# Which of four tiles the first of the two final plain stores takes

## Chip, cores and metric

One core of one Trainium2 chip. The metric is the device time of one execution in microseconds (us), the median of several runs. Every granted clock is 1.0 (the kernel has no matmul). The profile's own span is about 1.8 us shorter than the time of the run.

## The reference

The input is `x`, 16 x 64 x 64 x 64 float32. All 15 x 15 windows of 8 x 8 at a stride of 4 are copied out, 59.0 MB in all:

```python
for i in range(n_h):
    for j in range(n_w):
        h_start = i * stride
        w_start = j * stride
        result[:, i, j] = x[:, :, h_start:h_start + window_size, w_start:w_start + window_size].copy()
```

## The kernel before

The input is loaded once. Then windows are put together by ACT and DVE (copies, and shuffles for windows that cross a partition) in a tile of 128 partitions by 16 KB, and stored. There is room for four such tiles, G0 to G3. They are dealt in turn by a counter:

```python
NG = 4
G = [gpool.tile([P, C, WS, WS], f32, name=f"G{n}") for n in range(NG)]
...
at = 0

def tile_():
    nonlocal at
    at += 1
    return G[(at - 1) % NG]
```

Most stores are indirect (`scatter`, issued by POOL; each partition's 16 KB row goes to a row of the output that an index names; rows with an index out of bounds are left out). A crossing store (s = 2) leaves out 16 of the 64 rows of one half of the partitions, and `turn` says which half:

```python
def unit(j, s):
    nonlocal crossed
    g = tile_()
    ...
        turn = crossed % 2
        crossed += 1
        fill(g, turn, s, j, 0, HP, (act, act))
        fill(g, 1 - turn, s + 1, j, 0, HP, (dve, dve))
        scatter(g, (idx_hi, idx_lo)[turn], j, s)
...
while plain:
    for w in cross[:3]:
        unit(*w)
    cross = cross[3:]
    unit(*plain.pop(0))
```

The last column of windows (j = 14) is left over: two half-full tiles, 64 rows each, which go out by plain stores, four of 16 rows (256 KB) for each tile. SP issues all four of the first tile and two of the second; ACT issues the other two:

```python
j = NW - 1
tile_()
for s in range(2):
    g = tile_()
    cols = slice(j * ST, j * ST + WS)
    for y in range(NY):
        d = slice(QP + y * QP, QP + (y + 1) * QP)
        for ch, copy in enumerate((act, dve)):
            f = slice(ch * HP + y * QP, ch * HP + (y + 1) * QP)
            copy(out=g[d, ch * CL : (ch + 1) * CL, :, :], in_=L[f, :, s * ST : s * ST + WS, cols])
    g_q = g.rearrange("p c r w -> p (c r w)")
    for q in range(HQ):
        free((nc.sync, nc.scalar)[s * q % 2].dma_start(out=o_q[q * NSLOT + s, j], in_=g_q[QP + q : QP + q + (B - 1) * HQ + 1 : HQ]))
```

Of the kernel before, what the change touches and what calls it, by code (L numbers as in the profile page):

```python
# [10 lines left out]
def kernel(  # L11
# [106 lines left out]
    def free(st):  # L118
        tc.declare_no_dep(st.ins, group="stores", reason="each store writes rows of its own")
        tc.add_to_no_dep_group("stores", st.ins)  # L120
# [31 lines left out]
# [6 lines that stand above are left out]
# [43 lines left out]


    j = NW - 1
    tile_()
    for s in range(2):
        g = tile_()
        cols = slice(j * ST, j * ST + WS)
        for y in range(NY):
            d = slice(QP + y * QP, QP + (y + 1) * QP)
# [6 lines that stand above are left out]
# [35 lines left out]
```

## Time and profile before

| | before |
|---|---|
| time, median of the first 3 runs | 191.89 us |
| span in the profile | 190.1 us |
| DVE busy / ACT busy / POOL busy | 63% / 68% / 26% |
| share of DMA in the chain that ended last | 84% |
| moved over the span | 75.81 MB, 399 GB/s mean |

No compute engine is near its limit; transfers are.

### The profile page before, as it was taken

How to read it: one execution, taken by the hardware profiler on the slowest of the kernel's cores; microseconds unless marked ns; L12 is line 12 of the kernel's file. 1: busy time of each engine (PE TensorE's matmuls, PEld its weight loads, DVE VectorE, ACT ScalarE, POOL GpSimd, SP SyncE). 2: the span in 40 equal slices, each digit the busy share in tenths (PEclk: the TensorE clock that was granted, in tenths of full speed). 3: DMA queues.
4: the chain of work that ended last, by engine and by line, in shares of the span. 5: the costliest groups of instructions: out<-in, count | busy, mean ns of one | idle time of the engine just before them, and what ended most of it. 6: DMA issues, size and time to landing. Idle time of an engine off the chain costs nothing.

```text
span 190.1 us, 481 instructions
## 1 busy us (share of the span) xinstructions
DVE 120.5 (63%) x160; ACT 130.0 (68%) x69; POOL 49.9 (26%) x50
## 2 busy tenths in 40 slices
DVE  4000007999998969877659586795877679552420
ACT  0000007999999989977779589797877979572750
POOL 7402203205535321522322222223122431210000
DMA  2999999999999999999999999999999999999974
GB/s 83 310 408 403 398 400 396 400 401 392 438 431 431 422 424 441 417 410 417 441 397 431 426 422 414 424 438 393 438 414 417 428 424 424 405 434 410 421 331 197
DMA packets 11156, 75.81 MB, mean 399 GB/s; under 512 B 3456, under 2 KB 3456, under 8 KB 7552
## 3 DMA queue, kind: packets, MB, share of 16 engines
q0 software_dynamic: 9040, 66.34, 84.7%
q1 hardware_dynamic: 2048, 8.91, 12.0%
q10 hardware_dynamic: 64, 0.52, 0.7%
q14 instruction: 4, 0.03, 0.0%
HBM read 16.78 MB, written 62.91 MB: 419 GB/s over the span
## 4 chain that ended last, share of the span: by engine, by line
DMA 84%; DVE 6%; ACT 3%; POOL 2%; issue 1%; ACTq 0%; DVEq 0%; PEldq 0%
DMA out_dram<-G,idx_hi 30%; DMA L<-in_x_dram 20%; DMA out_dram<-G,idx 14%; DMA out_dram<-G,idx_y 13%; DMA out_dram<-G,idx_lo 7%; DVE G L166 4%; POOL L L58 2%; ACT G L212 2%; ACT G L143 1%; DVE G L146 1%; DVE G L145 0%; DVE G L143 0%; POOL pi L69 0%; ACTq L143 0%; DVEq L145 0%
## 5 line engine op out<-in xcount | busy, mean ns | idle before, releaser
L143 ACT COPY G<-L 64x2048 f32<-64x2048 f32 x46 | 87.2, 1896 | 17.0 <-DMA out_dram<-G,idx_hi 7.6
L166 DVE COPY G<-L 32x2048 f32<-32x2048 f32 x30 | 36.9, 1230 | 28.9 <-DMA L<-in_x_dram 25.9
L146 DVE STREAM_SHUFFLE G<-L 64x1024 f32<-64x1024 f32 x30 | 38.3, 1276 | 0.0
L166 ACT COPY G<-L 32x2048 f32<-32x2048 f32 x18 | 33.9, 1896 | 1.2 <-DMA out_dram<-G,idx_y 0.8
L145 DVE COPY G<-L 64x1024 f32<-64x1024 f32 x30 | 20.6, 688 | 16.4 <-DMA out_dram<-G,idx_hi 10.5
L143 DVE COPY G<-L 64x2048 f32<-64x2048 f32 x16 | 19.6, 1223 | 6.7 <-DMA out_dram<-G,idx 6.3
L166 ACT ACT_TABLE_LOAD x1 | 1.3, 1283 | 29.5 <-DMA L<-in_x_dram 29.5
L123 POOL DMA_INDIRECT out_dram<-G,idx_y x6 | 10.8, 1808 | 25.2 <-DVE G L166 24.1
L58 POOL DMA_DIRECT2D L<-in_x_dram x16 | 10.9, 695 | 24.1 <-DMA L<-in_x_dram 23.6
L123 POOL DMA_INDIRECT out_dram<-G,idx_hi x8 | 9.7, 1207 | 24.2 <-DVE G L146 12.3
L123 POOL DMA_INDIRECT out_dram<-G,idx_lo x7 | 8.0, 1144 | 29.4 <-DVE G L146 19.6
L123 POOL DMA_INDIRECT out_dram<-G,idx x8 | 10.2, 1270 | 18.0 <-ACT G L143 18.0
L212 ACT COPY G<-L 32x2048 f32<-32x2048 f32 x4 | 7.6, 1897 | 5.5 <-DMA out_dram<-G,idx_lo 4.5
L212 DVE COPY G<-L 32x2048 f32<-32x2048 f32 x4 | 4.9, 1220 | 8.2 <-DMA out_dram<-G,idx_lo 5.8
L72 DVE TENSOR_SCALAR tb<-pi 128x1 int32<-128x1 int32 x1 | 0.2, 155 | 1.0 <-POOL pi L69 1.0
L78 DVE TENSOR_TENSOR th<-tc,tq 128x1 int32<-128x1 int32 x2 | 0.3, 156 | 0.0
L75 DVE TENSOR_SCALAR th<-tc 128x1 int32<-128x1 int32 x2 | 0.3, 154 | 0.0
L69 POOL IOTA pi<- 128x1 int32 x1 | 0.1, 124 | 0.4 <-PEq L246 0.4
L146 DVE LOAD_MASK_SELECT G<-L x30 | 0.2, 6 | 0.0
L78 DVE CUSTOM_DVE_ANT_0 tb<-tb,th 128x2 uint16<-128x2 uint16 x1 | 0.2, 160 | 0.0
L78 DVE CUSTOM_DVE_ANT_0 idx_y<-idx_y,idx 128x2 uint16<-128x2 uint16 x1 | 0.2, 160 | 0.0
L78 DVE CUSTOM_DVE_ANT_0 idx<-tb,th 128x2 uint16<-128x2 uint16 x1 | 0.2, 159 | 0.0
(16 smaller groups left out, 2.2 us busy)
## 6 DMA issues: line engine op xcount, KB each, us to landing
L<-in_x_dram POOLq DMA_DIRECT2D x8, 1024.0 KB, 21.1
L<-in_x_dram SPq DMA_DIRECT2D x8, 896.0 KB
out_dram<-G SPq DMA_DIRECT2D x6, 256.0 KB
L<-in_x_dram POOLq DMA_DIRECT2D x8, 128.0 KB, 21.2
out_dram<-G ACTq DMA_DIRECT2D x2, 256.0 KB
out_dram<-G,idx POOLq DMA_INDIRECT x8, 14.7
out_dram<-G,idx_hi POOLq DMA_INDIRECT x8, 14.6
out_dram<-G,idx_lo POOLq DMA_INDIRECT x7, 12.9
```

What stands on the lines that cost most here:

```text
L58: eng.dma_start(out=L[p0 : p0 + QP - HQ + 1 : HQ, c0:c1, :, :], in_=x_v[ch, y, q, :, c0:c1, :])
L69: nc.gpsimd.iota(pi[:, :], pattern=[[0, 1]], base=0, channel_multiplier=1)
L72: nc.vector.tensor_scalar(out=d[:, :], in0=pi[:, :], scalar1=shift, scalar2=mask, op0=ALU.logical_shift_right, op1=ALU.bitwise_and)
L75: nc.vector.tensor_scalar(out=d[:, :], in0=a[:, :], scalar1=float(m), scalar2=None, op0=ALU.mult)
L78: nc.vector.tensor_tensor(out=d[:, :], in0=a[:, :], in1=b[:, :], op=op)
L123: st = nc.gpsimd.indirect_dma_start(out=o_v, out_offset=bass.IndirectOffsetOnAxis(ap=ix[:, 0:1], axis=0), in_=g.rearrange("p c r w -> p (c ...
L143: copy(out=g[d, cs, :, :], in_=L[f, :, s * ST : s * ST + WS, cols])
L145: copy(out=g[d, cs, 0:ST, :], in_=L[f, :, s * ST : RB, cols])
L146: nc.vector.stream_shuffle(out=g[d, cs, ST:WS, :], in_=L[f, :, 0:ST, cols], mask=nxt)
L166: (act if (2 * d + ch) % 3 == 0 else dve)(out=g[d * QP : (d + 1) * QP, ch * CL : (ch + 1) * CL, :, :], in_=L[f : f + QP, :, s * ST : s * S ...
L212: copy(out=g[d, ch * CL : (ch + 1) * CL, :, :], in_=L[f, :, s * ST : s * ST + WS, cols])
```

## The change

The intent is that the first plain fill should take the tile that comes free next, instead of letting that one go by, so that it doesn't wait. The tile that is passed over is now the one between the two plain fills, so the second fill keeps its tile.

```diff
     j = NW - 1
-    tile_()
     for s in range(2):
         g = tile_()
+        at += 1
```

## The prediction

> **What bounds the kernel now.** I read the page first, then the chain that ended last, then the timeline, the stretches and the DMA queues of the last 35 us, since the change touches nothing earlier: each engine's order of instructions is the same in both builds up to the last two fills.
>
> The chain of work that ended last, in its final part (start us, us, what):
>
> ```profile
> 164.83 14.61 DMA out_dram<-G,idx_hi
> ...
> 179.52 1.90 ACT G L212
> 181.44 1.90 ACT G L212
> ```
>
> The end hangs on one store landing, then on the second of the two plain fills (two ACT copies), then on its store, which the chain does not print: 183.34 to 190.1.
>
> To see who holds which tile I counted the allocations. Tiles are dealt in turn from four, by a counter. Nine uses go to the first nine fills, twenty to the loop, so the last four of the loop are use 25 (G1, idx_hi), 26 (G2, idx_lo), 27 (G3, idx_hi) and 28 (G0, idx). Use 29 (G1) is thrown away, the first plain fill is use 30 (G2), the second is use 31 (G3). The timeline (start us, busy us, engine, line, ..., the idle time before and its releaser):
>
> ```profile
> 155.90 1.24 POOL L123 DMA_INDIRECT out_dram<-G,idx_hi  x1 [3.06 <-ACT G L143]
> ...
> 160.95 0.96 POOL L123 DMA_INDIRECT out_dram<-G,idx_lo  x1 [3.81 <-DVE G L146]
> ...
> 164.83 0.97 POOL L123 DMA_INDIRECT out_dram<-G,idx_hi  x1 [2.93 <-DVE G L146]
> 166.41 3.82 ACT L143 COPY G<-L 64x2048 f32<-64x2048 f32 x2 [2.44 <-DMA out_dram<-G,idx]
> ...
> 170.50 0.96 POOL L123 DMA_INDIRECT out_dram<-G,idx  x1 [4.70 <-ACT G L143]
> 174.68 3.82 ACT L212 COPY G<-L 32x2048 f32<-32x2048 f32 x2 [4.45 <-DMA out_dram<-G,idx_lo]
> ...
> 178.52 7.26 SPq L215 DMA_DIRECT2D out_dram<-G  x6
> 179.52 3.82 ACT L212 COPY G<-L 32x2048 f32<-32x2048 f32 x2 [1.02 <-DMA out_dram<-G,idx_hi]
> ...
> 183.37 1.29 ACTq L215 DMA_DIRECT2D out_dram<-G  x2
> ```
>
> The reader is to see three things. ACT is idle for 4.45 us before the first plain fill, because it waits for G2 (store 26, issued 160.95, landed 174.64). The second plain fill starts when G3 (store 27, issued 164.83) lands at 179.44, and that wait doesn't name G1 or G2 at all. And SP issues six of the eight plain stores in one row, 178.52 to 185.78.
>
> Stretches of the tail (window, length, busy DVE, ACT, POOL, clock, DMA share, GB/s):
>
> ```profile
> 174.00:176.00 2.00, 1.27 (x2) 1.32 (x1) 0.00 (x0) 1.00 1.05 442
> 176.00:178.00 2.00, 1.17 (x1) 1.98 (x2) 0.00 (x0) 1.00 0.92 393
> 178.00:180.00 2.00, 0.47 (x1) 0.98 (x2) 0.00 (x0) 1.00 0.97 410
> 180.00:182.00 2.00, 1.97 (x2) 1.98 (x2) 0.00 (x0) 1.00 0.83 352
> 182.00:184.00 2.00, 0.00 (x1) 1.34 (x1) 0.00 (x0) 1.00 0.68 287
> 184.00:186.00 2.00, 0.00 (x0) 0.00 (x0) 0.00 (x0) 1.00 0.93 393
> 186.00:188.00 2.00, 0.00 (x0) 0.00 (x0) 0.00 (x0) 1.00 0.78 328
> 188.00:190.10 2.10, 0.00 (x0) 0.00 (x0) 0.00 (x0) 1.00 0.02 8
> ```
>
> Until 180 the transfers fill the 16 engines; after that they are not quite full, and the last 2.1 us are landing only. The queues in 180 to 182 (queue, packets, MB, share):
>
> ```profile
> q0 software_dynamic: 35, 0.46, 54.0%
> q1 hardware_dynamic: 31, 0.25, 29.3%
> ```
>
> This is how the plain stores (q1, issued by SP) and the indirect ones (q0, issued by POOL) share: 0.25 of 0.71 MB goes to q1.
>
> **What the Trainium skill says.** "DMA: Bandwidth & Descriptors", section "Queues, rings and completion order": each DMA engine goes round between the queues that have work, packet by packet. The trace agrees (q0 and q1 both move in 180 to 182). So an earlier plain store isn't put behind the queued indirect stores; it takes bandwidth from them. Same page, section "Why a DMA increments its semaphore by 16 and not by 1": a transfer has landed only when all of its engines have finished; so store 27's slowest engine counts. Here a store lands some 3 us after its bytes are through on average (worked out below). Same page, "Anatomy of one DMA": about 2 us of a transfer are fixed, mostly the receipt. The last 2.1 us at 8 GB/s agree. Same page, "Issuing engines are not separate DMA queues": issuing from several engines saves only issue time. So no bandwidth is gained here either.
>
> **The change part by part.** Removed: nothing. Added: nothing. The sums of bytes, copies and stores are equal. Moved: the first plain fill goes from use 30 (G2) to use 29 (G1). The second one stays on G3, since the counter is stepped once more after the first.
>
> (a) First fill. It now waits for store 25 instead of 26. Store 25 was issued at 155.90; with the usual 14.6 us of idx_hi to landing it lands near 170.5. (Stores 24 and 26 land at 166.37 and 174.64, so the middle is 170.5 too.) ACT is through with the fill before it at 166.41 + 3.82 = 170.23. So the first fill starts near 170.5 instead of 174.68, 4.2 us earlier, and SP issues its four stores from 174.4 instead of 178.52. The first packets followed the issue by about 1.4 us (178.52 to about 179.9 in the half-microsecond stretches): from 175.8. None of these 4.2 us is on the path to the end as such.
>
> (b) Second fill. It needs store 27. In 178 to 184 q0 moved 0.80 + 0.46 + 0.20 = 1.46 MB, all of it store 28's, whose size is 128 rows of 16 KB = 2.10 MB. So 0.64 MB of 28 had gone by 178, and the bytes of 27 were through on average at 178 - 0.64/0.41 = 176.4, yet it landed only at 179.44. From 175.8 the first plain store now takes its 0.125 MB per us (0.25 MB in 2 us, above). On the slowest engine 27 is still moving until about 177.5 to 178.5 (1 to 2 us of receipt before 179.44). That is 1.7 to 2.7 us by 0.125 = 0.2 to 0.34 MB put ahead, or 0.5 to 0.8 us at 0.41 MB per us; up to twice that if the slowest engine gets the unlucky share; less if most of the lag is receipt. I take +0.8 us, within 0 to 1.6. The second fill then ends at 184.15 instead of 183.34.
>
> (c) The end. Before, SP's fifth store waited its turn: filled 183.34, issued 183.77, and q1 still carried the first plain store until about 185.3. Now SP and q1 are free by then (174.4 + 5.1 us of four issues = 179.5), so the second store's issue and packets come 0.4 to 0.8 us sooner after its fill. I take -0.6 us.
>
> Sum: +0.8 - 0.6 = +0.2 us: 192.1 us.
>
> **The rivals.** First, the bytes simply move up and the end gets the gap. The tail from 178 moved 3.56 MB (the sum of the six stretches). At 0.415 MB per us it would take 8.6 us, ending at 186.6, plus 2.0 of landing: 188.6, so at most 1.5 us (0.8%) faster: 190.4 us. Against it: the second store can't start before store 27 lands, and the change doesn't bring that nearer; the gain is limited to (c). Second, the earlier store delays 27 by its whole size: 1.05 MB at 0.41 = 2.5 us, of which (c) gives back 0.6: 193.8 us, 1% slower. Against it: 27's bytes are mostly through by the time, and q1 gets only about a third. Third, nothing at all: 27's lag is receipt, and SP's backlog is harmless because the DMA engines share the end anyway: 191.9 us.
>
> **Range and chances.** The low end is no delay and 0.7 of (c): 191.2. The high end is a delay of 1.6 or somewhat more and little of (c): 193.2. Two per cent are 3.8 us; faster by that is more than the whole gap in the tail holds (1.5 us), slower by that is more than a delay by the store's whole size. So within 2% is nearly sure, 0.97; faster 0.01, slower 0.02.
>
> **What would show it.** Right: ACT's idle time before the first L212 copies shrinks from 4.45 us to under 0.6 and its releaser is idx_hi; SP's first plain store is issued near 174.4; the second pair of L212 copies starts at 179.5 to 181.1 still released by idx_hi, after a longer idle time of ACT; q1 moves about 1 MB in 176 to 182 and q0's share falls there; SP's last two issues follow the fill at once. Wrong: the second fill starts later than 181.5, which would mean that q1 takes more than a third or that the slowest engine decides; or the second store takes longer from issue to the end than the 6.8 us of before (183.34 to 190.1), with indirect bytes still in q0 then; or the first fill doesn't start by 171, so that store 25 landed later than worked out.

## The result, and the profile after

| | before | after |
|---|---|---|
| time, median of 6 runs each | 191.94 us (191.54 to 192.29) | 192.15 us (191.97 to 192.41) |
| ratio, after to before | | 1.0012, 95% interval 0.9998 to 1.0026 |

A ratio is the mean time of one kernel's runs over that of the other's in the same rounds, so it is not quite the ratio of the medians. Executions over 1.5% slower than the fastest of the same kernel are left out of the means. By the interval, 0.2 us slower is not told apart from nothing.

The same views as before, for the changed kernel. The chain that ended last (start us, us, what):

```profile
165.08 14.62 DMA out_dram<-G,idx_hi
...
179.78 1.90 ACT G L212
181.70 1.90 ACT G L212
```

It is the chain of before, 0.26 us later in all. Those 0.26 us arose ahead of the change: store 27 (idx_hi, G3) was issued at 165.08 instead of 164.83, where both kernels still have the same instructions. It took 14.62 us to land, against 14.61. The spans of the two profiles differ by 0.55 us; the other 0.29 us came after the last packet (0.54 us to the last landing instead of 0.37, and 1.04 us from there to the end instead of 0.92).

The timeline (start us, busy us, engine, line, and the idle time before with its releaser):

```profile
170.76 0.96 POOL L123 DMA_INDIRECT out_dram<-G,idx  x1 [4.71 <-ACT G L143]
171.31 3.81 ACT L212 COPY G<-L 32x2048 f32<-32x2048 f32 x2 [0.82 <-DMA out_dram<-G,idx_hi]
...
175.15 10.28 SPq L215 DMA_DIRECT2D out_dram<-G  x6
179.78 3.82 ACT L212 COPY G<-L 32x2048 f32<-32x2048 f32 x2 [4.66 <-DMA out_dram<-G,idx_hi]
...
183.62 1.83 ACTq L215 DMA_DIRECT2D out_dram<-G  x2
```

ACT's idle time of 4.45 us ahead of the first plain fill has shrunk to 0.82; that fill starts at 171.31 instead of 174.68. The idle time has moved: ACT now stands 4.66 us ahead of the second plain fill, which waits for the same landing as before.

Now the queues (q0 holds the stores that POOL issues, q1 those of SP, q10 those of ACT): what moved in 176 to 178, 178 to 180 and 180 to 182 (the first line is the first of these stretches, and so on; queue, packets, MB, share of the engines):

```profile
q0 software_dynamic: 56, 0.92, 107.9%
...
q0 software_dynamic: 52, 0.72, 84.8%
q1 hardware_dynamic: 6, 0.10, 11.5%
...
q1 hardware_dynamic: 60, 0.54, 64.2%
q0 software_dynamic: 26, 0.29, 34.8%
```

The plain store was issued at 175.15, yet nothing of it moved before 178; its first packet is at 179.71. In 180 to 182 the plain stores take the larger part: before, q1 moved 0.25 MB there and q0 0.46; now 0.54 and 0.29. It was issued 3.4 us sooner (175.15 against 178.52), but its first packet came only 0.3 us sooner (179.71 against 180.00): the rest was spent in the queue. And when it did move, it moved in the place of store 28 (the last indirect one, G0). Time from issue to landing of the indirect stores issued after 160, before and then after (the largest is store 28's in the changed kernel):

```profile
DMA to landing us min/median/max: 13.7/14.6/14.6
```

```profile
DMA to landing us min/median/max: 13.7/14.6/16.4
```

Store 28 lands at 187.16 instead of 185.09. The plain store goes ahead of it, and the end does not move.

### The profile page after: what moved, and what is told of

Read it like the earlier page. It is cut to its first block, busy times and chain, and to the rows that moved or that the text cites. A ratio compares the mean times of both kernels' runs of the same rounds, so it can differ in the third digit from the quotient of the medians.

```text
span 190.6 us, 481 instructions
## 1 busy us (share of the span) xinstructions
DVE 120.5 (63%) x160; ACT 130.0 (68%) x69; POOL 49.8 (26%) x50
## 4 chain that ended last, share of the span: by engine, by line
DMA 84%; DVE 5%; ACT 4%; POOL 2%; issue 1%; ACTq 0%; DVEq 0%; PEldq 0%
DMA out_dram<-G,idx_hi 29%; DMA out_dram<-G,idx 22%; DMA L<-in_x_dram 21%; DMA out_dram<-G,idx_y 13%; DVE G L166 4%; ACT G L143 2%; POOL L L58 2%; ACT G L212 2%; DVE G L143 0%; POOL pi L69 0%; ACTq L143 0%; DVEq L166 0%; PEldq L246 0%; ACTq L212 0%
```

## The experiments

The records of single packets explain the result; the theories come from them. They don't name the engine, but a full row of 16 KB takes 0.61 us, and rows that each start where another ended can be strung together. That all rows of such a string ran on one engine is inferred from these times; that store 27 lands 0.42 us after the row ahead of the string both times, and store 28 0.6 us after its last row in it, fits. Strung back from the last packet, with the queue in brackets (start times, us; where two engines' rows start within 0.02 us, the queue of one row was settled by the count of rows):

```
before, after store 27's last row on this engine:
179.02(q0) 179.63(q0) 180.24(q0) 180.84(q0) 181.45(q0) 182.06(q0) 182.66(q0) 183.27(q1)
183.88(q0) 184.50 185.11 185.72 186.34 186.96 187.57 188.17 (q1 or q10), last one ends 188.78
changed:
179.28(q0) 179.89(q1) 180.49(q0) 181.11(q0) 181.71(q1) 182.32(q0) 182.93(q0) 183.54(q1)
184.15(q0) 184.76(q0) 185.37(q1) 185.98(q0) 186.59 187.21 187.82 188.43 (q1 or q10), last one ends 189.04
```

Both times it is 16 rows: 8 of store 28, 4 of the first plain tile, 4 of the second. Both times 16 x 0.607 = 9.71 us and a little more pass, with no gap. Only the order differs.

**Theory A:** this one DMA engine, the last of the sixteen to finish, is never out of work; its number of rows sets the end. **Theory B**, as the chain of waits and the prediction had it: the end hangs on the second plain fill and the 6.8 us after it.

The most telling numbers of all runs are put together first (us from the span's start, each kernel's profiled execution; a store has landed with the sixteenth increment of its semaphore):

| run | second fill ends | store 28 lands | last packet ends | last landing | span |
|---|---|---|---|---|---|
| before | 183.34 | 185.09 | 188.78 | 189.15 | 190.1 |
| changed | 183.60 | 187.16 | 189.04 | 189.58 | 190.6 |
| e1 | 178.99 | 188.61 | 189.07 | 189.43 | 191.3 |
| e2 | 190.78 | 186.88 | 194.60 | 195.02 | 196.0 |
| e3 | 183.47 | 184.40 | 187.38 | 187.82 | 189.0 |
| e4 | 182.47 | 183.21 | 187.70 | 188.07 | 189.0 |
| e5 | 185.86 | 186.80 | 189.68 | 190.10 | 191.1 |
| e7 | 182.44 | 185.82 | 187.89 | 188.26 | 189.3 |
| e8 | 183.33 | 185.08 | 188.15 | 188.70 | 189.8 |
| e9 | 185.15 | 186.79 | 188.96 | 189.32 | 190.4 |
| e10 | 187.47 | 187.18 | 191.29 | 191.72 | 192.8 |

(In e6 POOL issues all stores; its own last landing is the last of all, 188.95, span 192.0.)

**e1: no tile passed over, second fill on G2.**

```diff
-    tile_()
     for s in range(2):
         g = tile_()
```

> No tile is skipped: the first plain fill takes G1 (as in the changed kernel), the second G2 instead of G3, so the second fill no longer waits for store 27 and ends about 4.6 us sooner (near 179.0 instead of 183.5). Theory A, one DMA engine of the sixteen is the last to finish and has work without a gap from before 160 to the end, so that only the number of its rows counts: no change of the time, 191.7 to 192.2. Theory B, the end hangs on the second plain fill and the 6.8 us after it: the end comes forward until the bytes bind, about 190.4 (1.5 us faster).

Measured: 192.99 us against 192.01 of the kernel before (ratio 1.0049, interval 1.0037 to 1.0061). 1.0 us slower. The timeline of e1:

```profile
171.33 7.66 ACT L211 COPY G<-L 32x2048 f32<-32x2048 f32 x4 [0.81 <-DMA out_dram<-G,idx_hi]
...
175.17 7.76 SPq L214 DMA_DIRECT2D out_dram<-G  x6
179.02 2.23 ACTq L214 DMA_DIRECT2D out_dram<-G  x2
```

Both plain fills now run without a break, and the second is done at 178.99, 4.6 us sooner than in the changed kernel. Theory B wanted 1.5 us for that; B falls. The last packet ends at 189.07, as in the changed kernel (189.04), which is theory A. But the time rose, which A did not foresee: after the last landing, 189.43, it took another 1.9 us to the end, where it takes 0.9 to 1.2 otherwise (e6 aside). POOL closes with a drain, which begins after its last issue; of the instructions on the closing line, this is POOL's drain (nanoseconds, shortest, median and longest; first and last start, us) before, in the changed kernel and in e1:

```profile
L246 POOLq DRAIN  x3: 51/105/16710, 170.3 to 189.8; - x3
```

```profile
L246 POOLq DRAIN  x3: 51/105/18517, 170.5 to 190.3; - x3
```

```profile
L245 POOLq DRAIN  x3: 51/105/19937, 170.6 to 191.0; - x3
```

The longest of the three is the one meant. It ends at 170.27 + 16.71 = 186.98 before, at 189.05 in the changed kernel and at 190.50 in e1: each time 1.89 us after store 28 landed (185.09, 187.16, 188.61). In the first two it is over while SP still waits for landings; in e1 SP is done at 189.57 and waits for POOL. So there is a second way to the end: the landing of POOL's last store, plus 1.9, plus 0.8 of closing steps (190.50 to 191.29). By the string of rows of e1, only two plain rows follow store 28's last row on the slowest engine, so six, instead of four, come ahead of it.

**e2: second fill on G0**, which store 28 has to free.

```diff
-    tile_()
     for s in range(2):
         g = tile_()
+        at += 2
```

> First fill on G1, second on G0, so it waits for store 28 instead of 27 and starts near 187.2 instead of 179.6. Here the slowest engine runs dry between the end of store 28 (about 186.6) and the packets of the second plain store (about 192.5). Theory A: the end is those packets plus 4 rows of 0.607 us and 1.6 us, a span near 196.6, time near 198. Theory B: 187.2 + 3.9 + 6.8 = a span near 197.9, time near 199.5. A miss of both would be a time below 195.

Measured: 197.89 us (ratio 1.0312, interval 1.0297 to 1.0327). Theory A's number, 198. Here the engines had run dry, so this run gives the shortest way from the second fill to the end: 190.78 to 196.0 is 5.2 us. In the kernel before it was 6.8. That fill therefore had some 1.5 us to spare.

**e3: the first plain tile not stored** (wrong; rows of the output are missing).

```diff
         for q in range(HQ):
+            if s == 0:
+                continue
```

> The kernel before without the four stores of the first plain fill (the fills stay): wrong result on purpose. Theory A: the slowest engine has 4 rows of 0.607 us less, 2.4 us, but then waits some 0.9 us for the second store: 1.5 us faster, 190.4. Theory B: the second fill starts and ends as before and only SP's backlog of 0.4 us goes: 191.5 or more.

Measured: 190.68 us (ratio 0.9925, interval 0.991 to 0.9939), 1.4 us faster though the second fill ended no sooner (183.47). As A said: 4 rows fewer; the slowest engine is through with store 28 at 184.00 and stands idle until 184.88. Theory B had 191.5 or more.

**e4: halves of the crossing windows swapped.**

```diff
-            turn = crossed % 2
+            turn = 1 - crossed % 2
```

The Trainium skill ("DMA: Bandwidth & Descriptors", section "The descriptor swizzle") gives the engine of a partition in a store of 128: eight engines for partitions 0 to 63, the other eight for 64 to 127. The trace agrees that there are two groups of eight. These are the sixteen increments of store 27's semaphore before and in e4 (us):

```
before: 175.44 175.50 175.51 175.53 175.56 175.58 175.59 175.63 | 178.51 178.63 178.65 178.66 178.68 178.70 178.76 179.44
e4:     176.74 176.81 176.82 176.86 176.87 176.89 176.90 176.92 | 177.39 177.40 177.44 177.54 177.59 177.60 177.67 178.37
```

One group is 3 us behind the other before (0.6 us in e4), and one engine of it another 0.7 us. Of the 15 crossing stores, 8 spare one half 2 rows per engine and 7 the other; if the kernel before gives the larger number of rows to the group that is late anyway, swapping takes 2 rows from it.

> The kernel before with the halves of the crossing windows swapped, so that 8 of the 15 crossing stores leave out the other half's rows. The result stays right. Theory A: the engines of the half that finishes last, the slowest among them, get 2 rows of 16 KB fewer in all (6 instead of 8 in one store), 1.2 us: 190.7, if the other half, which then has 2 rows more, still ends sooner. Theory B: store 27 lands up to 1.2 us sooner on its slowest engine, so also about 190.7. If it is unchanged, the row counts of the engines don't decide.

Measured: 190.98 us (ratio 0.9948, interval 0.9935 to 0.9961), 1.0 us faster, right result. The late group came forward by 1.1 us, the other went back by 1.3, and the last packet ended 1.08 us sooner. Both theories said so, and it is the best correct version found. It also rules out that the sum of bytes sets the end: that sum is the same here as before.

**e5: the first plain fill and its stores ahead of the last indirect store.**

```diff
+        if len(plain) == 1:
+            last(0)
         unit(*plain.pop(0))
-    j = NW - 1
     tile_()
-    for s in range(2):
-        ...
+    last(1)
```

(`last(s)` is the body of the final loop.)

> The kernel before with the first plain fill and its four stores moved ahead of the last indirect store (G0 for the plain fill, G1 for the last indirect one, G3 for the second plain fill as before). The plain packets should now reach the engines near 175, while store 27 is still moving. Theory A (the slowest engine is never out of work, its number of rows is the same): store 27 lands about 1.2 us later (2 plain rows of 0.607 us get in between) and the second fill with it, but the time stays at 191.7 to 192.3. Step (b) of the prediction taken as the path to the end: the delay of 1.2 us shows in the time, about 193.1.

Measured: 192.99 us (ratio 1.005, interval 1.0035 to 1.0065), so A's number is a miss. The other number, 193.1, was nearly hit, but not by the sum that it came from. Here the plain store does come while store 27 moves: issued at 170.35, it moves 0.38 MB in 174 to 176, and 27 lands at 181.97, issued at 164.99: 17.0 us instead of 14.6. The delay is 2.4 us, twice what was expected (four rows, not two), and it took the second fill beyond its spare time of some 1.5 us. The queue q1 in 174 to 176, the second fill, and a stretch near the end of e5:

```profile
q1 hardware_dynamic: 30, 0.38, 44.3%
```

```profile
182.04 3.82 ACT L204 COPY G<-L 32x2048 f32<-32x2048 f32 x2 [7.08 <-DMA out_dram<-G,idx_hi]
```

```profile
186.00:187.00 1.00, 0.00 (x0) 0.00 (x0) 0.00 (x0) 1.00 0.00 0
```

In 186 to 187 nothing moves at all: the engines are out of work, theory A's condition no longer holds, and the end is the fill plus 5.2 (185.86 + 5.2 = 191.1, the span). So the mechanism of step (b) of the prediction exists. The change just doesn't set it off.

**e6: all eight plain stores issued by POOL.**

```diff
-            free((nc.sync, nc.scalar)[s * q % 2].dma_start(...))
+            free(nc.gpsimd.dma_start(...))
```

> The kernel before with all eight plain stores issued by POOL, so they stand in q0 behind store 28, and the last store to land is one of POOL's own. If POOL's closing drain ends 1.9 us after its last landing, as the four traces so far have it, then the span is that landing plus 2.65 us instead of plus 0.95: with a last landing near 189.2, a span near 191.9 and a time near 193.6. If the drain means nothing, the time is that of the kernel before, 192.0.

Measured: 193.99 us (ratio 1.0105, interval 1.0088 to 1.0122). The last landing, 188.95, is 0.2 us sooner than before, the span ends 1.9 us later. POOL's closing drain (begun at 184.73, 6.43 us) ends 2.2 us after that landing. So it was paid in both runs in which POOL's own store landed so late; this confirms what e1 showed.

**e7: the changed kernel with e4's edit.**

> The changed kernel (first plain fill on G1, second on G3) with the halves of the crossing windows swapped as in the earlier run, where that gave 1.03 us on the kernel before. Theory A: the same gain, about 191.0 to 191.2, as the tile again moves nothing off the slowest engine. If the change of tile is worth something once the engines finish closer together: below 190.7. If store 28 is displaced so far that POOL's drain ends last: above 191.4.

Measured: 191.22 us (ratio to the kernel before 0.9961, interval 0.9947 to 0.9975), 0.75 us faster. No gain of the tile on top of e4's is to be seen: the interval overlaps with that of e4 (0.9935 to 0.9961). It was run at another time.

**e8: one of the first tile's four plain stores left out** (wrong).

```diff
         for q in range(HQ):
+            if s == 0 and q == 0:
+                continue
```

> The kernel before without one of the four stores of the first plain fill: wrong result on purpose. It is one row of 16 KB on each engine. Theory A: the slowest engine still has no gap, so exactly one row fewer, 0.6 us: 191.4. Theory B (second fill and what follows it): no change, 191.9 to 192.1.

Measured: 191.73 us (ratio 0.9987, interval 0.9973 to 1.0), 0.25 us faster. The last packet ends 188.15 instead of 188.78, so one row of 0.61 us did come off the slowest engine. But A's number for the time, 0.6, is a miss. The last landing comes 0.55 us after its last packet (0.37 before), and it isn't the store that SP looks at last: SP then goes through four waits instead of one, 0.06 us each. That accounts for 0.18 + 0.18 us. By its interval the gain in time only just differs from nothing; the firmer sign is the last packet, which moved by a row while the fill stayed at 183.33.

**e9 and e10: the changed kernel with the second fill's ACT copies done twice**, one of them in e9, both in e10 (right results).

```diff
-            for ch, copy in enumerate((act, dve)):
+            for ch, copy in enumerate((act, dve) + (act,) * (s == 1 and y < 1)):   # e10: y < 2
+                ch %= 2
```

> The changed kernel with one ACT copy of the second plain fill done twice (the same bytes; the result stays right), so that fill ends 1.9 us later, near 185.5. The runs in which the engines had run dry ended 5.2 us after the second fill: 185.5 + 5.2 = a span of 190.7, against 190.6 without the extra copy. Theory A, the fill has some 1.8 us to spare: 192.1 to 192.6 (0 to 0.4 us slower than the changed kernel's 192.15). Theory B, the fill is the path to the end: 194.0.

> The same with both ACT copies of the second plain fill done twice, 3.8 us later, near 187.4. Theory A: the first 1.8 us are free and the other 2.0 are paid, a span of 187.4 + 5.2 = 192.6, time 194.2 to 194.4. Theory B: all 3.8 us are paid, 195.9.

The second fill in the timelines of e9 and of e10:

```profile
179.41 5.74 ACT L213 COPY G<-L 32x2048 f32<-32x2048 f32 x3 [4.67 <-DMA out_dram<-G,idx_hi]
```

```profile
179.81 7.66 ACT L213 COPY G<-L 32x2048 f32<-32x2048 f32 x4 [4.66 <-DMA out_dram<-G,idx_hi]
```

Measured: e9 192.59 us, ratio to the kernel before 1.0034 (1.002 to 1.0048); e10 194.48 us, 1.0126 (1.011 to 1.0141). The changed kernel itself stood at 1.0012. (e9's profiled run, the one in the table, is its fastest.) So the first 1.9 us of delay cost 0.0034 - 0.0012 = 0.22%, 0.4 us, and the next 1.9 us cost 1.9 (194.48 - 192.59). The fill had some 1.5 us to spare in the changed kernel; beyond that it is paid in full. Theory A's numbers were 192.1 to 192.6 and 194.2 to 194.4; B's 194.0 and 195.9.

## Why the prediction was right, and where it was not

The number, 192.1 us, came out. Two terms of the sum, +0.8 and -0.6 us, did not, and they nearly cancelled: that the number was hit so closely is luck. What held is the bound, that the gap in the tail (1.5 us) is less than 2% (3.8 us).

- *(a), the first fill starts near 170.5 and nothing of the 4.2 us is on the path.* Right but for the size. It started at 171.31, as store 25 landed at 171.23 (its slowest engine last; 15.07 us after its issue instead of the usual 14.6), and SP issued at 175.15 instead of 174.4, later by 0.26 us of the run's own shift and by that landing. So it was 3.4 us early, not 4.2.
- *(b), store 27 lands 0.8 us later.* Wrong: 14.62 us against 14.61. The step that failed is "the first packets followed the issue by about 1.4 us ... from 175.8". The 1.4 us of before were read off engines that were just running out of indirect rows: there the plain packets began at 180.00, 1.5 us after the issue, where the last row of q0 ended. On the engines that still had rows of q0, they came 4.5 to 4.8 us after it even before the change (183.06 to 183.32). In the changed kernel all are such engines: 175.15 to 179.71 is 4.6 us, and by then store 27 was in. e5 shows that the delay does come, 2.4 us of it, when the store is issued 4.8 us earlier still. On the slowest engine seven rows of q0 begin between the issue and the first plain row, in both kernels. Why a plain store waits so long at a busy engine stays open. That it waits for the end of the indirect store in progress does not fit: before the change the slowest engine took a plain row between two rows of store 28.
- *Two readings behind (b)* were wrong too. The share of q1 in 180 to 182 isn't one engine's turn-taking: half of the engines were through with store 28 (its increments at 180.36 to 180.53) and moved plain rows from 180.00 on, while the other half moved store 28 alone and had their first plain rows only at 183.06 to 183.31. And the receipt of store 27 on the slowest engine was not 1 to 2 us: its last row there ended at 179.02, 0.42 us before it landed.
- *(c), -0.6 us because SP and q1 are free.* Wrong. SP did issue the second tile's stores at once (183.62, fill ended 183.60, against 0.43 us after it before), but the way from there to the end took 7.0 us, not less than 6.8. The engine that ends last was busy with what had been pushed back, store 28's rows, instead of the first plain tile's.
- *What bounds the end.* The prediction followed the chain of waits to the second fill. e1 (fill 4.6 us sooner, last packet not sooner), e3 and e8 (rows taken away, fill unmoved, end sooner), and e9 (fill later, 1.5 us of it free) show that it was the rows of the slowest engine. The third rival, "the DMA engines share the end anyway", is what happened, and its number was 191.9.
- *The rivals with numbers.* A gain of up to 1.5 us did not come, but for another reason than the one given: e1 brought the second fill forward and it did not come either. A delay of 2.5 us by the store's whole size did not come for the reason of (b); e5 shows nearly all of it, 2.4 us, once the stores do meet.
- *The signs to look for.* ACT's idle time shrank (0.82 us; I had said under 0.6), the second fill started at 179.78, inside 179.5 to 181.1. q1 did move some 0.9 MB up to 184 (0.10 + 0.54 + 0.23), but from 179.7 on and not from 176. Of the three signs named for "wrong", two were there: the first fill didn't start by 171, as store 25 landed later than worked out, and the second store took longer than 6.8 us to the end with indirect bytes still in q0 (7.0 us; q0 moved 0.21 MB in 184 to 186). A second fill later than 181.5 was not.

Three ways to the end fit all twelve traces: the slowest engine's last row plus 1.3 to 1.7 us, the second fill plus 5.2 us where the engines ran dry (e2, e5, e9; 5.3 in e10, 5.5 in e3), and POOL's last landing plus 2.7 us (e1; 3.0 in e6); whichever is last. The first two are fits with a spread of up to 0.4 us, more than the change itself made. The change moved nothing off the first. It ate most of the slack of the third (187.16 + 2.7 = 189.9 of 190.6), and e1 went over.

## What to carry to other kernels

When transfers fill the engines to the end, as here, a fill that starts sooner may only change the order of the queue; ask how many rows the last engine still has to move, not only which wait the chain names. Count rows per engine, not in total: here one half of the partitions skipped rows in 8 stores and the other in 7, and giving the extra skip to the half that is late was worth 1.0 us. And look at which engine issued the store that lands last: where it was POOL's (e6), or POOL's landed 0.8 us before the last (e1), POOL's closing drain set the end.

## What the Trainium skill lacked or had wrong

- "DMA: Bandwidth & Descriptors", "Specifications", states a first-byte latency of about 0.6 us for stores issued from SP or ACT. Here, at engines with nothing to do, the first packet came 1.2 to 1.3 us after the start of the issuing instruction, which is 0.65 to 0.8 us after its end (e2, e3, e5); so that figure about fits, if it counts from there. What the page doesn't have is the 4.5 to 5.2 us at engines with indirect rows queued (before, changed, e1, e2, e5). The turn-taking by packets of its section "Queues, rings and completion order" shows only after that: then mostly one plain row to two indirect ones (179.28 to 185.98 on the slowest engine of the changed kernel).
- Same page, "Anatomy of one DMA", which is about transfers that POOL issues, has about 2 us of fixed cost, mostly the receipt. The prediction took the last 2.1 us for that, and the trace doesn't agree: the last row (SP's) ended at 188.78, its landing came 0.37 us later, and 0.92 us were closing steps of the engines. POOL's stores landed 0.4 us (store 27) and 0.6 us (store 28) after their last rows on the slowest engine.
- No page that I read has the wait of POOL's closing drain: it ended 1.89 us after POOL's last store had landed (before, changed, e1, e5) and 2.2 us in e6, where that store is a plain one, and it set the end in e1 and e6.
- Same page, "Latency and other measured facts", says that two of the sixteen engines are usually slower. Here one was: 0.7 to 1.3 us behind its group at each of the last five indirect stores of before (store 27: 179.44 against 178.76). Which one it is the records don't say. That a group of eight falls behind by what an index leaves out is on no page: from the eighth increment to the ninth, the gap between the groups is 2.9 us at store 27 before and 0.5 us in e4; at store 26, when both halves had skipped the same number of rows, it is 1.59 us before and 1.65 in e4, so that this much of the lag has another cause, which no run shows.
